# Expert-gate one-hots with two tokens innermost instead of four, in a two-block transformer kernel on one core

## The chip, the cores and the metric

The kernel runs on one core of a Trainium2 chip. It is one program for two transformer blocks, 256 tokens of width 1024 in float32. The metric is the device time of one execution in microseconds (us), the median of three runs.

## What is computed

The first block has two gated feed-forward parts around a mixer (block-sparse attention and retention), the second a mixer (RWKV-7 and mLSTM) and then PEER, a retrieval of single-neuron experts. The change lies in PEER. Cut to what matters:

```python
def _peer(h, w_q, sub_keys, u_emb, v_emb):
    q = (tok @ w_q).reshape(n_tok, 8, 2, 128)
    s = jnp.einsum('nhpc,hpkc->nhpk', q, sub_keys)
    s_top, i_top = lax.top_k(s, 16)
    cand = s_top[:, :, 0, :, None] + s_top[:, :, 1, None, :]
    cand_idx = i_top[:, :, 0, :, None] * 128 + i_top[:, :, 1, None, :]
    best, pos = lax.top_k(cand.reshape(n_tok, 8, 256), 16)
    expert = jnp.take_along_axis(cand_idx.reshape(n_tok, 8, 256), pos, axis=-1)
    gate = jax.nn.softmax(best, axis=-1)
    act = gelu(einsum('tkd,td->tk', u_emb[expert], tok)) * gate
    return einsum('tk,tkd->td', act, v_emb[expert])
```

Each token picks 16 experts in each of 8 heads, 128 of 16384 in all. An expert's number is a pair (a, b) of numbers below 128.

## The kernel before

The kernel does not gather experts. It computes the product of every token with all 16384 rows of `peer_u`, applies GELU, multiplies each product by the token's gate for that expert (zero for most), and multiplies the result by all of `peer_v`.

A float32 weight is split on its way in: a DMA from SyncE's queue brings `raw`, ScalarE rounds it to `whi` (L111), GpSimd and VectorE subtract to get the remainder `wlo` (L113, L115). A product is then three matmuls, L132 to L134, with 256 moving columns each. `pair` does two blocks of 128 experts: 48 such matmuls.

`retrieve` runs in three parts. First come the scores (L1400 to L1411). The searches for the top 16 (`half`, `whole`, L1322 to L1336) and the picks of the winners' numbers (`gates`, `pick`, `turn`, L1338 to L1374) stand in a list of background work, `self.bg`, of which `wload` issues an item after each weight. Third, as soon as the numbers are there (`finish`), the loop over `peer_u` (L1420) also makes the gates: `IT` holds for each token, transposed, the numbers a and b and the gate of its 128 selections, one selection per partition, and `ix` the same in fp16, the gate in two halves (high and low).

For each group of `GT` = 4 tokens, `onehots` (L1385) makes with four VectorE operations of 128x512 elements the one-hots of a and of b (L1391: compare a constant `io`, which counts 0 to 127, with `ix`), and then the one-hot of b times each half of the gate (L1393). Both inputs and the output are fp16. The tile `oh` lies as [what, group, number 0 to 127, token], the token innermost. For each token two matmuls (L1440) sum the product of a's one-hot (the weights, stationary) and b's scaled one-hot (moving, 128 columns) over the selections into `pg`: the 128x128 gates of this token. So there are 512 such gate matmuls, 8 for each group, and their operands step over `oh` by four elements. VectorE (L1443) multiplies the gates into `act`; ScalarE (L1444) copies those for experts still to come. `oh` has two buffers, so VectorE can make a group's one-hots only when the gate matmuls of the group two before are done.

A scheduler sets the order on each engine from a cost estimate of each instruction and from priorities; weights have a lead (`LEAD`). The order of instructions around the change is its result.

Of the kernel before, what the change touches and what calls it, by code (L numbers as in the profile page):

```python
# [12 lines left out]
F16 = mybir.dt.float16  # L13
# [17 lines left out]
GT = 4  # L31
# [36 lines left out]
class K:  # L68
# [406 lines left out]
    def mixer1(self, cx, p, a, b, gate):  # L475
# [101 lines left out]
        onsa = self.new_split(p, [128, 4, T], "on")  # L577
        G = range(2)
        for tt in range(2):
# [6 lines left out]
            for m in range(4):  # L586
                for g in G:
                    nc.tensor.matmul(sc[:, g, m * 16:m * 16 + 16], qh(g, m), kk[64 * g:64 * g + 64, 512:528],
                                     start=m == 0, stop=False, skip_group_check=True)
            mc = self.masks[:, 256 + 16 * tt:272 + 16 * tt]  # L590
            for g in G:
                nc.tensor.matmul(sc[:, g, 0:64], self.idb, mc[:, None, :].to_broadcast([128, 4, 16]), start=False, stop=True,
# [12 lines left out]
            for m in range(4):  # L605
                sc = ps2.tile([128, 2, 512], F32, name="sc")
                for g in G:
                    k = kk[64 * g:64 * g + 64, 0:512].rearrange("p (b k) -> p b k", b=2)
                    nc.tensor.matmul(sc[:, g, 0:2 * n].rearrange("p (b k) -> p b k", b=2), qh(g, m), k[:, :, 0:n],
                                     start=True, stop=False)  # L610
                for g in G:
                    nc.tensor.matmul(sc[:, g, 0:2 * n].rearrange("p (b k) -> p b k", b=2)[:, :, n - 128:n], self.idb,
# [4 lines left out]
                nc.vector.tensor_scalar(mx, mx, -0.125, None, op0=OP.mult)  # L617
                for g in G:
                    for br in range(2):
# [665 lines left out]
    def retrieve(self, act, tok, raws, pre):  # L1285
        nc, A, tc = self.nc, self.A, self.tc
        NEG = -3.0e38
        with ExitStack() as c1:
            pool = lambda n, b, **k: c1.enter_context(tc.tile_pool(name=n, bufs=b, **k))
            keep, pp = pool("pk", 1), pool("pk2", 2)  # L1290
# [8 lines left out]
            def view(n, dt=F32):  # L1299
                self.at += n  # L1300
                x = flat[:, self.at - n:self.at]
                return x if dt == F32 else x.bitcast(dt)
# [12 lines left out]
            iof = view(128)  # L1315
            nc.sync.dma_start(iof, A["iota"])

            io = keep.tile([128, 128, 4], F16, name="io")
            nc.vector.tensor_copy(io, iof[:, :, None].to_broadcast([128, 128, 4]))
            self.ready = False  # L1320

            def top16(v, i, src, n, z):  # L1322
# [56 lines left out]
                nc.vector.tensor_copy(ix[:, 2, :], IT[:, 2, :])  # L1379
                nc.vector.tensor_sub(ix[:, 3, :], IT[:, 2, :], ix[:, 2, :])  # L1380

            G = GT // 4
            shape = [128, G, 128, 4]

            def onehots(t0):  # L1385

                oh = pp.tile([128, 4, G, 128, 4], F16, name="oh")
                x = lambda i: ix[:, i, t0:t0 + GT].rearrange("p (g t) -> p g t", g=G)[:, :, None, :].to_broadcast(shape)
                iota = io[:, None, :, :].to_broadcast(shape)
                for i in range(2):  # L1390
                    nc.vector.tensor_tensor(oh[:, i], iota, x(i), op=OP.is_equal)  # L1391
                for i in (3, 2):
                    nc.vector.tensor_mul(oh[:, i], oh[:, 1], x(i))  # L1393
                return oh
# [24 lines left out]
            done = 0  # L1419
            for j in range(0, 128, 2):  # L1420
                ps = self.pair(A["peer_u"], j, tok, PU if self.ready else PQ).rearrange("p (j t) -> p j t", j=2)
                a = act[:, j:j + 2, :]
                if done < T:
                    nc.scalar.activation(a[:, :, done:], ps[:, :, done:], AF.Gelu)
                if done:
                    g = pp.tile([128, 2, T], F32, name="ge", tag="q")
                    nc.scalar.activation(g[:, :, 0:done], ps[:, :, 0:done], AF.Gelu)
                    nc.vector.tensor_mul(a[:, :, 0:done], a[:, :, 0:done], g[:, :, 0:done])
                J = j + 2
                if self.ready and JA is None:  # L1430
                    JA = J
                todo = 0 if JA is None else T * (J - JA) // (JB - JA) // GT * GT if J < JB else T
                while done < min(todo, T):
                    if done % GT == 0:
                        oh = onehots(done)
                    pg = psG.tile([128, 4, 128], F32, name="pg")
                    g = done % GT // 4
                    for i in range(4):
                        for l in (3, 2):
                            nc.tensor.matmul(pg[:, i, :], oh[:, 0, g, :, i], oh[:, l, g, :, i], start=l == 3, stop=l == 2)  # L1440
                    pv = pg.rearrange("p t j -> p j t")
                    a = act[:, 0:J, done:done + 4]
                    nc.vector.scalar_tensor_tensor(a, pv[:, 0:J, :], 2.0 ** -10, a, op0=OP.mult, op1=OP.mult)  # L1443
                    nc.scalar.activation(act[:, J:128, done:done + 4], pv[:, J:128, :], AF.Copy, scale=2.0 ** -10)  # L1444
                    done += 4
# [199 lines left out]
```

## Time and profile before

| | us |
|---|---|
| median of 3 runs | 1840.1 (1837.5 to 1842.22) |
| the profiled execution, its own time | 1844.43 |
| span of the profiled execution | 1842.6 |
| TensorE (PE) busy, matmuls | 1732.9 |
| VectorE (DVE) busy | 1254.4 |
| ScalarE (ACT) busy | 889.5 |
| GpSimd (POOL) busy | 833.8 |

The span runs from the first to the last instruction of one profiled execution; its own time contains 1.8 us more. PE stands for the matmuls, PEld for the weight loads, which overlap with them. A matmul's duration in the profile holds its passage through the array and overlaps with that of its neighbours: how fast matmuls follow one another is read from their starts. L1440 is line 1440 of the kernel.

### The profile page before, as it was taken

The numbers are of one execution on the slowest core, as the hardware profiler recorded it, in microseconds if no ns is written. First come the engines' busy times: TensorE is split into PE (matmuls) and PEld (weight loads), VectorE is DVE, ScalarE is ACT, GpSimd is POOL, SyncE is SP. The second block draws the span as 40 slices with busy tenths as digits, with TensorE's granted clock in tenths as the row PEclk, the third lists the DMA queues.
The fourth block names the chain that finished last, engine by engine and source line by source line (L and its number), as shares of the span: only waits on it lengthen the run. The fifth ranks groups of instructions, "written<-read, shape, count | busy, mean of one in ns | idle before, by whom it ended". The sixth has DMA issues, their size and how long they took to land.

```text
span 1842.6 us, 36282 instructions
## 1 busy us (share of the span) xinstructions
PE 1732.9 (94%) x13856; PEld 1608.6 (87%) x13856; DVE 1254.4 (68%) x2559; ACT 889.5 (48%) x1416; POOL 833.8 (45%) x625
## 2 busy tenths in 40 slices
PE   5999989999999989899998979999999999999998
PEld 4999977689899989799998878999999988888886
DVE  8886588777744586865588997777788633434344
ACT  4444444645544456644554334444444445555554
POOL 3444522224555556413444655333333456666664
PEclk9999999999999999999999989999999999999999
DMA  7887778536555645303454435545555566666664
GB/s 264 290 319 243 209 271 282 188 115 198 159 184 180 189 146 153 101 15 106 157 179 143 136 120 164 158 151 159 151 151 157 172 196 192 185 190 186 190 186 137
DMA packets 95928, 325.77 MB, mean 177 GB/s; under 512 B 10505, under 2 KB 18313, under 8 KB 95242
## 3 DMA queue, kind: packets, MB, share of 16 engines
q1 hardware_dynamic: 95466, 322.93, 55.5%
q8 instruction: 108, 1.77, 0.4%
q14 instruction: 66, 0.54, 0.1%
q10 hardware_dynamic: 288, 0.52, 0.1%
HBM read 321.32 MB, written 2.10 MB: 176 GB/s over the span
## 4 chain that ended last, share of the span: by engine, by line
PE 64%; DVE 10%; issue 3%; ACT 2%; POOL 2%; DMA 0%; POOLq 0%; ACTq 0%; DVEq 0%; SPq 0%
PE vacc L1469 20%; PE acc L134 12%; PE acc L133 12%; PE acc L132 12%; PE pg L1440 3%; DVE wlo L115 2%; PE pt L908 1%; POOL wlo L113 1%; ACT whi L111 1%; DVE nt L264 1%; DVE rt L753 1%; PE acc L154 0%; DVE cv L1203 0%; PE pt L469 0%; PE pc L1409 0%
## 5 line engine op out<-in xcount | busy, mean ns | idle before, releaser
L113 POOL TENSOR_TENSOR wlo<-raw,whi 128x256 fp32r<-128x256 f32 (+4 forms) x526 | 764.4, 1455 | 847.0 <-ACT whi L111 794.8
L111 ACT CAST whi<-raw 128x1024 fp32r<-128x1024 f32 (+2 forms) x530 | 550.7, 1041 | 434.5 <-PE acc L133 189.2
L134 PE MATMUL acc<-uh,wlo 128*128 128x256 f32 x2352 | 667.7, 284 | 25.2 <-POOL wlo L113 22.1
L115 DVE TENSOR_TENSOR wlo<-raw,whi 128x768 fp32r<-128x768 f32 (+5 forms) x530 | 484.6, 916 | 286.2 <-ACT whi L111 285.2
L132 PE MATMUL acc<-uh,whi 128*128 128x256 f32 x2352 | 670.5, 285 | 1.5 <-DVE gf L439 1.3
L133 PE MATMUL acc<-ul,whi 128*128 128x256 f32 x2352 | 666.7, 283 | 1.3 <-DVE ul L177 1.3
L134 PEld LDWEIGHTS acc<-uh,wlo 128*128 128x128 f32 x2352 | 449.1, 191 | 31.2 <-POOL wlo L113 25.2
L132 PEld LDWEIGHTS acc<-uh,whi 128*128 128x128 f32 x2352 | 451.8, 192 | 3.8 <-DVE gf L439 2.0
L133 PEld LDWEIGHTS acc<-ul,whi 128*128 128x128 f32 x2352 | 450.2, 191 | 3.2 <-DVE ul L177 1.7
L1469 PE MATMUL vacc<-whi,ah 128*128 128x512 f32 x512 | 162.7, 399 | 3.9 <-ACT ah L176 3.9
L1469 PE MATMUL vacc<-whi,al 128*128 128x512 f32 x512 | 162.5, 398 | 0.0
L1469 PE MATMUL vacc<-wlo,ah 128*128 128x512 f32 x512 | 162.4, 398 | 0.0
L177 DVE TENSOR_TENSOR al<-act,ah 128x256 fp32r<-128x256 f32 x128 | 54.7, 429 | 133.9 <-PE vacc L1469 133.4
L176 ACT CAST ah<-act 128x256 fp32r<-128x256 f32 x128 | 52.4, 411 | 158.3 <-PE vacc L1469 156.3
L1469 PEld LDWEIGHTS vacc<-whi,ah 128*128 128x128 f32 x512 | 97.1, 190 | 26.8 <-ACT ah L176 4.1
L1469 PEld LDWEIGHTS vacc<-wlo,ah 128*128 128x128 f32 x512 | 97.1, 190 | 23.1 <-POOL wlo L113 0.2
L1469 PEld LDWEIGHTS vacc<-whi,al 128*128 128x128 f32 x512 | 97.0, 190 | 22.8
L347 DVE SCALAR_TENSOR_TENSOR junk<-aw,cb 128x1024 bf16<-128x1024 f32 x72 | 95.1, 1321 | 11.7 <-DMA aw<-in_ada_w_dram 11.2
L1391 DVE TENSOR_TENSOR oh<-io,ix 128x512 f16<-128x512 f16 x128 | 73.8, 616 | 42.9 <-PE pg L1440 42.9
L132 PE MATMUL acc<-gh,whi 128*128 128x256 f32 x352 | 97.2, 276 | 0.0
L133 PE MATMUL acc<-gl,whi 128*128 128x256 f32 x352 | 97.2, 276 | 0.0
L134 PE MATMUL acc<-gh,wlo 128*128 128x256 f32 x352 | 97.2, 276 | 0.0
(502 smaller groups left out, 2362.1 us busy)
## 6 DMA issues: line engine op xcount, KB each, us to landing
raw<-in_peer_u_dram SPq DMA_DIRECT2D x128, 512.0 KB, 3.6
raw<-in_peer_v_dram SPq DMA_DIRECT2D x128, 512.0 KB, 4.2
raw<-in_ffn_w_in_dram SPq DMA_DIRECT2D x88, 512.0 KB, 3.8
raw<-in_w_in_dram SPq DMA_DIRECT2D x78, 512.0 KB, 3.6
aw<-in_ada_w_dram SPq DMA_DIRECT2D x72, 512.0 KB, 5.6
raw<-in_ffn_w_out_dram SPq DMA_DIRECT2D x32, 448.0 KB, 3.9
raw<-in_ffn_w_out_dram SPq DMA_DIRECT2D x16, 512.0 KB, 3.5
raw<-in_w_out_dram SPq DMA_DIRECT2D x16, 512.0 KB, 3.6
```

Source lines behind the costliest of these rows:

```text
L111: nc.scalar.copy(hi, t)
L113: nc.gpsimd.tensor_sub(lo[:, :pool], t[:, :pool], hi[:, :pool].bitcast(F32))
L115: nc.vector.tensor_sub(lo[:, pool:], t[:, pool:], hi[:, pool:].bitcast(F32))
L132: mm(out, w.hi, x.hi, start=start, stop=False)
L133: mm(out, w.hi, x.lo, start=False, stop=False)
L134: mm(out, w.lo, x.hi, start=False, stop=stop)
L176: self.nc.scalar.copy(hi, src)
L177: self.nc.vector.tensor_sub(lo, src, hi.bitcast(F32))
L347: nc.vector.scalar_tensor_tensor(self.junk, t, 1.0, self.cb, op0=OP.mult, op1=OP.mult, accum_out=acc)
L1391: nc.vector.tensor_tensor(oh[:, i], iota, x(i), op=OP.is_equal)
L1440: nc.tensor.matmul(pg[:, i, :], oh[:, 0, g, :, i], oh[:, l, g, :, i], start=l == 3, stop=l == 2)
L1469: nc.tensor.matmul(acc[2 * tt + d], x[:, ts], y[:, d * 512:(d + 1) * 512], start=j == 0 and x is a.hi and y is w.hi, stop=j == 127 and x i ...
```

## The change

The innermost dimension of the one-hots becomes two tokens instead of four. A group of 4 tokens (`GT` stays 4) is now two sub-groups of two: `oh` lies as [what, sub-group, number, token of the pair]. The constant `io` has two copies of each number in place of four, and the matmuls pick sub-group and token with `divmod`. Sizes and counts of the one-hot operations and of the matmuls stay; what a matmul steps over is two elements (4 bytes) instead of four (8 bytes), and `io` is read twice over by each compare.

```diff
-            io = keep.tile([128, 128, 4], F16, name="io")
-            nc.vector.tensor_copy(io, iof[:, :, None].to_broadcast([128, 128, 4]))
+            io = keep.tile([128, 128, 2], F16, name="io")
+            nc.vector.tensor_copy(io, iof[:, :, None].to_broadcast([128, 128, 2]))
...
-            G = GT // 4
-            shape = [128, G, 128, 4]
+            G = GT // 2
+            shape = [128, G, 128, 2]
...
-                oh = pp.tile([128, 4, G, 128, 4], F16, name="oh")
+                oh = pp.tile([128, 4, G, 128, 2], F16, name="oh")
...
-                    g = done % GT // 4
                     for i in range(4):
+                        g, t = divmod(done % GT + i, 2)
                         for l in (3, 2):
-                            nc.tensor.matmul(pg[:, i, :], oh[:, 0, g, :, i], oh[:, l, g, :, i], start=l == 3, stop=l == 2)
+                            nc.tensor.matmul(pg[:, i, :], oh[:, 0, g, :, t], oh[:, l, g, :, t], start=l == 3, stop=l == 2)
```

On PE, ScalarE and SyncE's queue the order of instructions is the same as before, and on VectorE from the first one-hot (L1391) on. On VectorE it differs ahead of that, from the cast of `io` on. There VectorE did in this order (MAX, MAX_INDEX and MATCH_REPLACE are the searches, L115 a weight's remainder; `act` holds their scratch space):

```order
L115 TENSOR_TENSOR wlo<-raw,whi 128x256
L1319 CAST io<-act 128x512
L1326 MAX act<-act 128x8
L115 TENSOR_TENSOR wlo<-raw,whi 128x256
L1327 MAX_INDEX act<-act 128x8
L1323 MAX act<-act 128x8 x2
```

Now it does, on the same engine at the same place:

```order
L115 TENSOR_TENSOR wlo<-raw,whi 128x256
L1319 CAST io<-act 128x256
L1326 MAX act<-act 128x8
L1323 MAX act<-act 128x8
L115 TENSOR_TENSOR wlo<-raw,whi 128x256
L1327 MAX_INDEX act<-act 128x8
```

The cast has half the elements, and one search operation stands ahead of the next weight's remainder. Such exchanges of a weight's remainder with one or two searches follow in a dozen places. On VectorE at the start of the picks the difference reads (L1363 compares positions, L1349 to L1352 end the softmax of the gates):

```order
 L1349 CAST act<-act 128x128
 L1351 RECIPROCAL act<-act 128x8
+L1363 TENSOR_TENSOR act<-act 128x512
 L115 TENSOR_TENSOR wlo<-raw,whi 128x256
 L1352 TENSOR_TENSOR act<-act 128x128
```

A pick's first operation has moved ahead of a weight's remainder, and the picks behind it are dealt out among the weights by other steps.

## Rows read from the trace of the kernel before

**Rows 1.** The page, part 1: busy us, share of the span, instructions

```profile
PE 1732.9 (94%) x13856; PEld 1608.6 (87%) x13856; DVE 1254.4 (68%) x2559; ACT 889.5 (48%) x1416; POOL 833.8 (45%) x625
```

**Rows 2.** Windows: length, busy PE PEld DVE ACT POOL (instructions), PEclk, DMA share, GB/s

```profile
980.00:1060.00 80.00, 71.49 (x567) 69.00 (x565) 78.14 (x366) 31.64 (x38) 46.38 (x34) 0.96 0.43 133
1060.00:1127.00 67.00, 50.72 (x367) 49.02 (x367) 61.57 (x112) 24.08 (x30) 39.83 (x24) 0.87 0.41 127
1127.00:1443.00 316.00, 315.61 (x2726) 312.75 (x2725) 248.96 (x459) 141.60 (x247) 106.20 (x95) 1.00 0.52 156
```

**Rows 3.** The chain that ended last, of the stretch 1127 to 1443 us

```profile
by line: PE acc L134 26.9%; PE acc L132 26.8%; PE acc L133 26.8%; PE pg L1440 19.2%; DVE wlo L115 0.3%; DVE oh L1393 0.1%; issue 0.0%
```

**Rows 4.** Waits, 1127 to 1443 us: total us, times, longest

```profile
DVE oh L1391 <- PE pg L1440: 42.9, 43, 1.8
...
DVE wlo L115 <- ACT whi L111: 23.7, 28, 2.0
```

**Rows 5.** Timeline of PE around three bursts: start, us, what (merged where alike)

```profile
1139.53 1.11 PE L1440 MATMUL pg<-oh 128*128 128x128 f16 x8
...
1255.69 0.28 PE L133 MATMUL acc<-ul,whi 128*128 128x256 f32 x1
1255.81 0.28 PE L134 MATMUL acc<-uh,wlo 128*128 128x256 f32 x1
1255.92 1.11 PE L1440 MATMUL pg<-oh 128*128 128x128 f16 x8
1256.79 0.37 PE L132 MATMUL acc<-uh,whi 128*128 128x256 f32 x1
1256.99 0.28 PE L133 MATMUL acc<-ul,whi 128*128 128x256 f32 x1
...
1441.20 2.06 PE L1440 MATMUL pg<-oh 128*128 128x128 f16 x16
```

**Rows 6.** All that touches the tile oh: duration ns min/median/max

```profile
L1440 PEld LDWEIGHTS <-oh x512: 112/117/138, 1139.5 to 1442.8; 128*128 128x128 f16 x171
L1440 PE MATMUL pg<-oh x512: 283/297/303, 1139.5 to 1443.0; 128*128 128x128 f16 x171
L1391 DVE TENSOR_TENSOR oh<-io,ix x128: 406/426/965, 1127.5 to 1436.3; 128x512 f16<-128x512 f16 x128
L1393 DVE TENSOR_TENSOR oh<-oh,ix x128: 403/412/976, 1130.9 to 1439.5; 128x512 f16<-128x512 f16 x128
```

**Rows 7.** Timeline of PE: the 16-bit mask matmuls, operands side by side

```profile
287.10 0.20 PE L592 MATMUL sc<-masksb,idb 128*128 128x64 bf16 x1
...
287.14 0.20 PE L592 MATMUL sc<-masksb,idb 128*128 128x64 bf16 x1
...
287.37 0.28 PE L134 MATMUL acc<-uh,wlo 128*128 128x256 f32 x1
...
290.49 0.28 PE L612 MATMUL sc<-masksb,idb 128*128 128x256 bf16 x1
...
290.61 0.27 PE L612 MATMUL sc<-masksb,idb 128*128 128x256 bf16 x1
...
290.85 0.28 PE L134 MATMUL acc<-uh,wlo 128*128 128x256 f32 x1
```

**Rows 8.** Line 612: the weight load of a side-by-side 16-bit operand

```profile
L612 PEld LDWEIGHTS <-idb x16: 95/97/99, 290.5 to 343.3; 128*128 128x128 bf16 x16
```

**Rows 9.** Line 1363: an f32 operation of the same width on VectorE

```profile
L1363 DVE TENSOR_TENSOR act<-act x16: 675/682/2317, 1070.0 to 1119.2; 128x512 f32<-128x512 f32 x16
```

**Rows 10.** Line 1319: the cast of the constant io

```profile
L1319 DVE CAST io<-act x1: 2055/2055/2055, 983.4 to 983.4; 128x512 f16<-128x512 f32 x1
```

**Rows 11.** Waits of PE, 980 to 1127 us: total us, times, longest

```profile
PE acc L134 <- POOL wlo L113: 21.6, 9, 4.4
```

**Rows 12.** Timeline of PE: 64-column f32 matmuls of the second mixer

```profile
819.24 0.87 PE L908 MATMUL pt<-idn,X 64*64 64x64 f32 x24
```

**Rows 13.** Line 908: their weight loads

```profile
L908 PEld LDWEIGHTS pt<-idn,X x256: 129/135/135, 801.2 to 822.9; 64*64 64x64 f32 x128
```

## The prediction

> **What bounds the kernel now.** I read the page's totals first: PE is busy 94% of the span [rows 1]. That share is an average, so next comes the table of windows [rows 2]. The reader should look at two of its stretches. From 1127 to 1443 us, where the expert gates are applied, PE is busy 315.6 of 316.0 us at a granted clock of 1.00 (the 2.4 GHz level), VectorE 249.0, and the DMA share is 0.52. From 980 to 1127 us, the top-16 searches and picks, VectorE is busy 78.1 of 80.0 and 61.6 of 67.0 us while PE has gaps and a clock of 0.96 and 0.87. So the one-hot stage is bound by PE, the stage ahead of it mostly by VectorE. The chain of waits of the one-hot stage says the same: four lines of PE make up all but half a per cent of it, and the gate matmuls (L1440) alone are 19.2%, or 60.7 us, 0.119 us for each of 512 [rows 3]. The other engines wait for PE or for each other there [rows 4]. A nanosecond off each gate matmul is therefore half a microsecond off the kernel.
>
> **Why the gate matmuls cost that.** The timeline of PE shows them in 45 bursts, the first at 1139.53 us and the last at 1441.20, of 8 or 16 matmuls each [rows 5]. A burst of 8 lasts 1.11 us and one matmul alone 0.297 [rows 5, 6], so the seven spacings are (1.11 - 0.297) / 7 = 0.116 us; the burst of 16 gives (2.06 - 0.297) / 15 = 0.1175. I take 0.117. The f32 matmuls around them start every 0.11 us with 256 moving columns; the gate matmuls have 128 columns and take as long. The trace has 16-bit matmuls with operands that lie side by side: with 64 columns two start 0.04 us apart, with 256 columns 0.12 us [rows 7]. That is 0.08 us for 192 columns, 0.42 ns each, plus a fixed 0.013. For 128 columns this line gives 0.013 + 128 x 0.417 ns = 0.066 us. So the gate matmuls take 0.051 us more than their columns explain. What is special about them is the step: neighbouring columns of a one-hot lie 4 elements, 8 bytes, apart. A gate matmul thus reads across 128 x 8 = 1024 bytes per partition, exactly what an f32 matmul reads with 256 x 4, and their spacings agree. That is my reason to think that the bytes passed over set the pace, not the columns.
>
> **The change, part by part.**
> 1. *Matmuls.* Counts and order on PE stay; the step falls from 8 to 4 bytes, so the 128 columns lie within 512 bytes. Four bytes per column is what the f32 matmuls have at 0.42 ns per column. The price of a 16-bit matmul with a 4-byte step is in no row. Bounds: from below half an f32 spacing, 0.057 us; from above no gain, 0.117. I take 0.066, the value of the side-by-side rows, since those are the nearest in type. Inside the bursts there are 512 - 45 = 467 spacings: 467 x 0.051 = **23.8 us**, all on the chain.
> 2. *Back to f32.* From the start of a burst's last matmul (1255.92 + 7 x 0.117 = 1256.74) to the second f32 matmul (1256.99) pass 0.25 us [rows 5]; behind the side-by-side 16-bit pairs it is 0.23 and 0.24 [rows 7]. 45 x 0.015 = **0.7 us**. The first spacing of a burst belongs to the f32 matmul ahead of it and stays.
> 3. *Weight loads.* A one-hot load lasts 117 ns [rows 6], a side-by-side one 97 [rows 8]. Whether that matters is rival B.
> 4. *VectorE, one-hots.* 256 operations of 128x512 as before, median 426 and 412 ns [rows 6]; only the patterns change, with rows of two elements instead of four. I cost that at nothing: an operation of this width at one element per cycle takes 675 ns [rows 9], so these run at two, and a pair is still adjacent. From the first one-hot on the order of VectorE is the same. The cover is PE: with its stage at 316 - 24.5 = 291.5 us, VectorE has 249.0 busy and 23.7 of waits for weight casts [rows 4], 272.7 together. The 42.9 us in which it waited for gate matmuls to free a one-hot buffer are what shrinks. 19 us of room are left.
> 5. *The iota cast.* It halves from 512 elements, now 2.06 us [rows 10], in the stage that VectorE bounds: between 0 and 1.0 us gained. I take 0.
> 6. *The order ahead.* The shorter cast lets the scheduler move the weight subtractions (L115) by a place or two among the searches, and one pick (L1363) ahead of one of them. PE waited there 21.6 us for weights in 9 waits, the longest 4.4 [rows 11]. One wait more or one fewer is up to 4.4 us either way; I take 0.
>
> The sum is 23.8 + 0.7 = **24.5 us**. The profiled execution took 1844.4 us and would take 1819.9; the median of the three runs is 4.3 us lower, and against it I predict 1840.1 - 24.5 = **1815.6 us**. DMA has room for a stage 8% shorter: its share there is 0.52.
>
> **A rule that speaks against it.** The gate matmuls now are at 0.117 us where side-by-side columns give 0.066. The Trainium skill, page "SBUF — State Buffer", section "Door 1: The DMA port swizzle", says that two hits on a 16-byte line suffice for full bandwidth, so that 8 elements of bf16 can be stepped over for free. By that rule a step of 4 already costs nothing and the change brings nothing: 1840.1 us. The trace does not agree that the present step is free, unless something else slows these matmuls; so the rule is rival C. The same notes, page "TensorE: Matmul & The Clock Gate", section "Back-to-back issue gap", put pairs of load and matmul with 128 columns at about 81 ns; by that the first term would be an estimated 467 x 0.036 = 16.8 us.
>
> **The rivals.**
> *B, the weight load takes over.* In a burst the loads last 117 ns, the same as the spacing; if each matmul must wait for a whole load, the spacing falls only to the 97 ns of a side-by-side load: 467 x 0.020 = 9.3 us, 1830.8. Against it: 24 of the 64-column f32 matmuls run within 0.87 us, at most 36 ns each, while one load is 135 ns long [rows 12, 13]; but those alternate between two halves of the array, so it is not excluded.
> *C, no change.* Any step other than one, or fp16 itself, may run at half rate; nothing in the trace has a step of two. Then 1840.1 us, give or take the 4.4 us of term 6.
> *D, slower: VectorE drops to one element per cycle* because the repeated row is now only one pair long. Price: 675 - 412 = 0.26 us on each of 256 one-hot operations, 66.6 us. VectorE's 272.7 us become 339.3, more than the 316 of the stage: 1840.1 + 23.3 = 1863.4 us. It decides from (291.5 - 272.7) / 256 = 73 ns extra per operation, where it begins to eat the gain; above (316 - 272.7) / 256 = 169 ns the kernel is slower than before. For it: no row of the trace shows rows of two 16-bit elements. Against it: rows of four run at full rate. The Trainium skill, page "Vector Engine (DVE) Microarchitecture Reference", section 5.1, says that two elements per partition do run at double rate and that a row read again and again does too; no run here shows it yet.
>
> **How the numbers follow.** The forecast has 0.62, B 0.14, C 0.14, D 0.10. A measurement of this kernel can tell about 0.3%, 5.5 us, from no change. The forecast and B are faster, and a small part of C by the order ahead: 0.77. The rest of C is the same: 0.13. D is slower: 0.10. The forecast's own range is 1810 (a spacing of 0.057, 4 us less, and a little from term 6) to 1824 (a spacing of 0.075 with one more weight wait). To leave out no more than 2 in 10, the range goes up over B and half of C: 1810 to 1841.
>
> **What would show it.** Right: 8 gate matmuls from first start to f32 restart in about 0.5 us instead of 0.87 [rows 5], spacings near 0.066, the one-hot stage near 291 us, their share of its chain near 12%, VectorE's wait for gate matmuls about halved with its operations still at 410 to 430 ns, one-hot loads under 117 ns. B shows as spacings of 0.097; C as 0.117; D as one-hot operations near 680 ns and PE waiting for weights from L115. Wrong altogether would be a stage no shorter although the spacings fell: then a VectorE or weight wait has taken their place.

## The result and the profile after

The changed kernel takes **1809.5 us** (median of 4 runs, 1807.8 to 1810.9) where the kernel before took 1840.3 beside it (median of 4, 1837.5 to 1842.2): a ratio of 0.982, 95% interval 0.980 to 0.984. The gain is 30.8 us; 24.5 had been forecast, and the time lies half a microsecond below the lower end of the range. The profiled execution took 1807.8 us, 1.7 under its median (the one before had been 4.1 over its own).

The page of the changed kernel opens with its span (1842.6 us before) and the busy time of the engines, which answers to [rows 1]:

```profile
span 1806.0 us, 36282 instructions
...
PE 1695.2 (94%) x13856; PEld 1575.8 (87%) x13856; DVE 1255.9 (70%) x2559; ACT 887.1 (49%) x1416; POOL 828.8 (46%) x625
```

The counts of instructions are those of before on every engine. PE is busy 37.7 us less, VectorE as long as before. Where that happened is in the windows (columns as in [rows 2]; the last window ends where the last burst now ends):

```profile
980.00:1060.00 80.00, 70.98 (x587) 68.58 (x585) 77.26 (x379) 33.20 (x41) 47.28 (x36) 1.00 0.46 141
1060.00:1127.00 67.00, 51.73 (x371) 50.17 (x370) 61.78 (x106) 24.01 (x30) 39.51 (x22) 0.87 0.41 126
1127.00:1413.00 286.00, 284.50 (x2718) 282.03 (x2717) 251.19 (x457) 138.58 (x245) 99.76 (x93) 1.00 0.56 172
```

The stage in which the gates are applied is over after 286 us instead of 316, at the same granted clock of 1.00, and PE is still busy in all but 1.5 us of it. The two search windows in front look as before, but for the clock of the first (1.00 instead of 0.96). So the stage shrank because its own bound shrank; no wait of PE went away, and only 1.3 us of waits came in its place. The tile of the one-hots [rows 6] shows on what:

```profile
L1440 PEld LDWEIGHTS <-oh x512: 96/97/102, 1139.1 to 1412.9; 128*128 128x128 f16 x171
L1440 PE MATMUL pg<-oh x512: 217/218/233, 1139.1 to 1413.0; 128*128 128x128 f16 x171
L1391 DVE TENSOR_TENSOR oh<-io,ix x128: 407/416/983, 1127.0 to 1409.0; 128x512 f16<-128x512 f16 x128
L1393 DVE TENSOR_TENSOR oh<-oh,ix x128: 404/410/1001, 1130.4 to 1411.7; 128x512 f16<-128x512 f16 x128
```

A gate matmul lasts 218 ns instead of 297, its weight load 97 instead of 117, and the one-hot operations of VectorE take 410 to 416 ns, where they took 412 to 426. In the timeline of PE (start, duration, what), around the burst that answers to the one at 1255.92 in [rows 5]:

```profile
1256.43 0.28 PE L134 MATMUL acc<-uh,wlo 128*128 128x256 f32 x1
1256.55 0.63 PE L1440 MATMUL pg<-oh 128*128 128x128 f16 x8
1256.99 0.36 PE L132 MATMUL acc<-uh,whi 128*128 128x256 f32 x1
1257.19 0.29 PE L133 MATMUL acc<-ul,whi 128*128 128x256 f32 x1
```

From the first gate matmul to the return of f32 pass 0.44 us instead of 0.87. Over all bursts, read from the starts of the single matmuls in the two traces, the 467 spacings inside bursts sum to 28.4 us where they were 54.7; the median spacing is 57 ns, against 118 (means 61 and 117). The chain of waits from 1139 to 1413 us and the waits from 1127 to 1413 us (us in total, times, longest) answer to [rows 3, 4]:

```profile
by line: PE acc L132 28.8%; PE acc L133 28.0%; PE acc L134 27.9%; PE pg L1440 10.3%; DVE oh L1391 1.4%; issue 1.1%; DVE oh L1393 0.9%; DVE act L1428 0.7%; DVE act L1443 0.6%; ACT whi L111 0.4%; DVE wlo L115 0.2%
```

```profile
DVE wlo L115 <- ACT whi L111: 21.6, 26, 1.7
DVE oh L1391 <- PE pg L1440: 12.3, 18, 1.0
```

The gate matmuls' share of the chain fell from 19.2% to 10.3%, 28.2 of 274 us. VectorE waits 12.3 us for a one-hot buffer instead of 42.9. Busy time and its wait for weights are 251.2 + 21.6 = 272.8 us of the 286.0: the room of a dozen microseconds is what is left before VectorE becomes the bound here. That room is an average over the stage, and near its end it is gone. From 1386 to 1400 us the chain runs over ScalarE and VectorE, and in the bursts at 1392.8 and 1399 us three spacings last 331, 466 and 332 ns, about 0.9 us lost to one-hots that come late (each time the next gate matmul starts some 50 ns behind the end of an operation of L1393):

```profile
1388.07 1.84 DVE oh L1391 x2
...
1395.04 1.29 DVE oh L1393 x2
```

```profile
1399.88 0.89 PE L1440 MATMUL pg<-oh 128*128 128x128 f16 x8 [0.25 <-DVE oh L1393]
```

The other traces with two tokens innermost in both operands (e0, e1, e4 and e9 below) have such pauses at the same place.

**Where the 36.6 us between the two profiled spans lie.** The first gate matmul starts at 1139.07 us instead of 1139.53: 0.5 us. From there to the last gate matmul 273.9 us pass instead of 303.4: 29.5 us. From there to the end 393.0 instead of 399.7: 6.7 us, in a part that the change does not touch. The median moved by 30.8 only, so these last 6.7 us call for another execution of the kernel before (experiment e6_before).

The 29.5 us of the stage divide, by the same starts, into 26.3 inside the bursts; 1.1 at the return to f32 (from the start of a burst's last matmul to the second f32 matmul 227 ns instead of 252, 44 times within the stage); and 2.1 in the f32 matmuls between the bursts, whose mean spacing fell from 114.8 to 113.8 ns. That last part was in no term of the sum. Here is a stretch between two bursts in each timeline, the kernel before first:

```profile
1243.02 0.28 PE L133 MATMUL acc<-ul,whi 128*128 128x256 f32 x1
1243.13 0.28 PE L134 MATMUL acc<-uh,wlo 128*128 128x256 f32 x1
...
1248.43 0.28 PE L134 MATMUL acc<-uh,wlo 128*128 128x256 f32 x1
```

The changed kernel:

```profile
1244.88 0.28 PE L134 MATMUL acc<-uh,wlo 128*128 128x256 f32 x1
1244.99 0.28 PE L132 MATMUL acc<-uh,whi 128*128 128x256 f32 x1
...
1249.98 0.28 PE L134 MATMUL acc<-uh,wlo 128*128 128x256 f32 x1
```

Before, 46 spacings take 5.41 us, 117.6 ns each; now 45 take 5.10 us, 113.3 each, for the same instructions at the same granted clock. A stretch of 48 f32 matmuls between two bursts keeps the one pace or the other to its end. Of the 44 stretches, 13 were slow before; 1 is now.

### The profile page after: what moved, and what is told of

It is laid out like the page before. It is cut to its first block, busy times and chain, and to the rows that moved or that the text cites. A ratio compares the mean times of both kernels' runs of the same rounds, so it can differ in the third digit from the quotient of the medians.

```text
span 1806.0 us, 36282 instructions
## 1 busy us (share of the span) xinstructions
PE 1695.2 (94%) x13856; PEld 1575.8 (87%) x13856; DVE 1255.9 (70%) x2559; ACT 887.1 (49%) x1416; POOL 828.8 (46%) x625
## 4 chain that ended last, share of the span: by engine, by line
PE 61%; DVE 15%; issue 3%; ACT 2%; POOL 2%; DMA 1%; POOLq 0%; ACTq 0%; DVEq 0%; SPq 0%
PE vacc L1469 20%; PE acc L132 11%; PE acc L133 11%; PE acc L134 11%; DVE wlo L115 3%; PE pg L1440 2%; PE pt L908 1%; POOL wlo L113 1%; ACT whi L111 1%; DVE act L1327 1%; DVE act L1325 1%; DVE act L1324 1%; DVE nt L264 1%; PE pt L469 1%; DVE act L1326 1%
## 5 line engine op out<-in xcount | busy, mean ns | idle before, releaser
L115 DVE TENSOR_TENSOR wlo<-raw,whi 128x768 fp32r<-128x768 f32 (+5 forms) x530 | 492.3, 930 | 280.9 <-ACT whi L111 279.8
L1469 PEld LDWEIGHTS vacc<-whi,ah 128*128 128x128 f32 x512 | 96.5, 189 | 24.5 <-ACT ah L176 4.1
L1391 DVE TENSOR_TENSOR oh<-io,ix 128x512 f16<-128x512 f16 x128 | 61.8, 521 | 12.6 <-PE pg L1440 12.3
```

What stands on the lines that cost most here:

```text
L115: nc.vector.tensor_sub(lo[:, pool:], t[:, pool:], hi[:, pool:].bitcast(F32))
L1469: nc.tensor.matmul(acc[2 * tt + d], x[:, ts], y[:, d * 512:(d + 1) * 512], start=j == 0 and x is a.hi and y is w.hi, stop=j == 127 and x i ...
```

## The experiments

Theory: the moving operand's step sets the pace of a gate matmul. Against it stood rival B (the pace is that of the weight load, whose operand changed its step too), the order ahead (the changed order on VectorE in front of the stage gives or takes a part), and, for the size, what exactly the step costs. Diffs are against the changed kernel.

**e0_after.** The changed kernel again, as the measure for the next three.

> The changed kernel once more, for a second profile beside the same runs of the kernel before. Median 1809.5 us, within 2 us. If the spacing of the 512-column matmuls of the value product (0.234 us in the profile before, 0.230 in the one after) belongs to the change, it is 0.230 again; if it is a matter of the single execution, it may stand anywhere from 0.226 to 0.234.

Measured: 1810.7 us (5 runs, 1807.5 to 1819.3), ratio 0.983 [0.981, 0.986] to the kernel before, which took 1841.9 beside it. From first to last gate matmul 274.0 us, median spacing 57 ns, 1 slow f32 stretch of 44: the stage in the trace after is typical. The 512-column matmuls of the value product are 230 ns apart again.

**e1_four_copies.** The constant `io` keeps four copies, so that its cast and the order of VectorE ahead are those of the kernel before; the one-hots have two tokens innermost.

```diff
-            io = keep.tile([128, 128, 2], F16, name="io")
-            nc.vector.tensor_copy(io, iof[:, :, None].to_broadcast([128, 128, 2]))
+            io = keep.tile([128, 128, 4], F16, name="io")
+            nc.vector.tensor_copy(io, iof[:, :, None].to_broadcast([128, 128, 4]))
...
-                iota = io[:, None, :, :].to_broadcast(shape)
+                iota = io[:, None, :, 0:2].to_broadcast(shape)
```

> Two tokens innermost in the one-hots, but the constant io keeps its four copies, so that the cast and the order on every engine are those of before. If the new order and the shorter cast are worth nothing, the time is that of the changed kernel, 1809.5 us. If the part of the gain that the gate matmuls do not explain comes from the searches, as the two traces suggest with some 3 us there, it is 1812 to 1814 us. Gate spacing 0.057 us in either case.

Measured: 1812.4 us (1809.0 to 1815.0), ratio 0.983 [0.981, 0.985]; the stage 274.1 us, spacing 57 ns. All but 1.7 us of the gain is there without the changed order ahead. The time lies in the band expected for a part from the searches, but these 1.7 us to e0_after lie within the scatter of both.

**e2_moving_two and e3_weights_two** part the two operands of the gate matmul. In e2 the weights (`oh[0]`) keep four tokens innermost and the moving operands have two, in e3 the other way round. `io` keeps four copies in both, so their measure is e1.

```diff
+                def lay(i):
+                    n = 4 if i == 0 else 2
+                    s = [128, 4 // n, 128, n]
+                    o = oh[:, i].rearrange("p (g k t) -> p g k t", g=4 // n, t=n)
...
-                        g, t = divmod(done % GT + i, 2)
+                        gw, tw = divmod(done % GT + i, 4)
+                        gm, tm = divmod(done % GT + i, 2)
...
-                            nc.tensor.matmul(pg[:, i, :], oh[:, 0, g, :, t], oh[:, l, g, :, t], start=l == 3, stop=l == 2)
+                            nc.tensor.matmul(pg[:, i, :], oh[0][:, gw, :, tw], oh[l][:, gm, :, tm], start=l == 3, stop=l == 2)
```

(e3: `n = 2 if i == 0 else 4`, and 2 and 4 exchanged in the two `divmod` lines.)

> Only the moving one-hots (of b) have two tokens innermost; the stationary ones (of a) keep four. If the step of the moving operand sets the pace, the spacing is 0.057 us with weight loads still near 0.115 us, and the time is that of the kernel with four copies of io. If the weight load sets it, the spacing stays near 0.115 us and the time near 1840 us.

> The mirror image: only the stationary one-hots have two tokens innermost, the moving ones keep four. If the step of the moving operand sets the pace, the spacing stays at 0.107 to 0.117 us though a load falls to 0.097, and the time is within 5 us of 1840. If the weight load sets it, the spacing is 0.057 to 0.066 us and the time that of the kernel with four copies of io.

The tile of the one-hots in e2, then in e3:

```profile
L1447 PEld LDWEIGHTS <-oh x512: 112/113/137, 1141.3 to 1416.5; 128*128 128x128 f16 x171
L1447 PE MATMUL pg<-oh x512: 217/221/253, 1141.3 to 1416.6; 128*128 128x128 f16 x171
```

```profile
L1447 PEld LDWEIGHTS <-oh x512: 95/116/120, 1143.1 to 1442.8; 128*128 128x128 f16 x171
L1447 PE MATMUL pg<-oh x512: 275/297/300, 1143.1 to 1443.0; 128*128 128x128 f16 x171
```

Measured: e2 1812.2 us (6 runs, 1805.5 to 1821.3), ratio 0.984 [0.981, 0.987]; e3 1836.1 us (8 runs, 1829.5 to 1837.7), ratio 0.995 [0.994, 0.997]. In e2 the loads take 113 ns, nearly as long as before, and the matmuls follow each other every 59 ns: a load twice as long as the spacing holds nothing up. In e3 the matmuls are back at a median spacing of 117 ns, and the loads beside them mostly at 116, not at the expected 97, although their own step is the short one. So the moving operand sets the pace and the load does not, and rival B falls. A load is long from either cause: from its own step of four beside quick matmuls (e2), or beside matmuls of a step of four (e3). e3 is not quite the kernel before, though: it gains 5.8 us. Its trace shows none of the 44 f32 stretches slow (e2: 5), some 2.5 us, and 1.0 us less inside the bursts (mean spacing 115.0). Its stage is 3.6 us shorter than that of the profile before; the other 2.2 us of the medians are not placed. Two tokens innermost in the weights alone thus have a small effect, and most of what the traces place of it lies in the f32 matmuls behind the bursts rather than in the gate matmuls.

**e4_steps.** Between the one-hot stage and the value product, bursts of 16 matmuls on zeros, each with one step of the moving or the weight operand; nothing reads their result. A few of the 16 bursts:

```diff
+            self.steps()
...
+            [mm(o[:, 0:128], w[:, 0:128], z[:, 0:128], start=True, stop=True) for _ in R]
+            [mm(o[:, 0:128], w[:, 0:128], z[:, 0:256:2], start=True, stop=True) for _ in R]
+            [mm(o[:, 0:128], w[:, 0:128], z[:, 0:384:3], start=True, stop=True) for _ in R]
...
+            [mm(o[:, 0:128], w[:, 0:128], z[:, 0:2048:16], start=True, stop=True) for _ in R]
...
+            [mm(o[:, 0:128], w[:, 0:2048:16], z[:, 0:128], start=True, stop=True) for _ in R]
```

> The changed kernel with bursts of 16 matmuls of zeros set between the gates and the value product (some 25 us more; they add nothing to the output): 128 fp16 columns, weights and moving operand each at steps of 1, 2, 3, 4, 6, 8 and 16 elements, and bf16 at steps of 2 and 4. If the bytes that the moving operand passes over set the pace (1024 bytes in 0.107 us), the spacings are 0.057, 0.057, 0.083, 0.110, 0.163, 0.217 and 0.430 us. If it is lines of 16 bytes, the first six are the same and step 16 is 0.217 us again. If any step over two runs at half rate, steps 3 to 16 are all near 0.110 us. With the weights stepped and the moving columns side by side the spacing stays at 0.057 us up to a step of 4 if the moving operand sets the pace. bf16 as fp16.

Measured: steps of 3, 4 and 6 gave 88, 116 and 171 ns, and bf16 at steps of 2 and 4 gave 58 and 116, so fp16 has no part in it. Steps of 8 and 16 gave 227 and 232, but the granted clock was 0.5 (the 1.2 GHz level) from 1454.4 to 1464.7 us, which takes in these two bursts, all but the start of the first, and the weights' steps of 2 and 4. PE had been busy without a gap when it fell. The bursts of steps 8 and 16, and a window in them (columns as in [rows 2]):

```profile
1453.98 3.81 PE L1465 MATMUL zo<-zz,zw 128*128 128x128 f16 x16
1457.61 3.89 PE L1466 MATMUL zo<-zz,zw 128*128 128x128 f16 x16
```

```profile
1454.50:1461.30 6.80, 6.80 (x31) 3.70 (x30) 0.00 (x0) 0.00 (x0) 0.00 (x0) 0.50 0.00 0
```

The first burst, at step 1, and most of the second ran at 0.5 as well, at 107 ns. So the run leaves open what the clock did to these spacings.

**e9_steps_full_clock.** The same with bursts of 12, each led by 24 matmuls of 512 columns that lie side by side.

```diff
+            R, mm = range(12), nc.tensor.matmul
+            [mm(o, w[:, 0:128], z[:, 0:512], start=True, stop=True) for _ in range(24)]
+            [mm(o[:, 0:128], w[:, 0:128], z[:, 0:128], start=True, stop=True) for _ in R]
+            [mm(o, w[:, 0:128], z[:, 0:512], start=True, stop=True) for _ in range(24)]
+            [mm(o[:, 0:128], w[:, 0:128], z[:, 0:256:2], start=True, stop=True) for _ in R]
...
```

> The bursts of zeros again (they add nothing to the output), 12 matmuls each, now with 24 side-by-side matmuls of 512 columns ahead of every burst, since in the first such run the granted clock fell to 0.5 at steps 8 and 16 and at two of the weight steps. At a clock of 1.0 throughout: if the pace is one 16-byte line in some 1.8 ns, moving steps 1, 2, 3, 4, 6, 8, 16 give 0.057, 0.057, 0.088, 0.116, 0.171, 0.227 and 0.23 us; if it is bytes, step 16 gives 0.43. If the 0.227 of step 8 came from the low clock, it is near 0.12 now. Weights at steps 2, 4, 8 and 16 with side-by-side moving columns: 0.057 to 0.062 us each if the weight load does not set the pace; up to 0.117 and more if it does.

The window of the bursts (columns as in [rows 2]):

```profile
1458.00:1540.00 82.00, 81.85 (x460) 42.74 (x458) 0.00 (x0) 0.00 (x0) 0.00 (x0) 1.00 0.00 1
```

The clock is 1.00 throughout. The bursts in the timeline of PE, in order: moving operand at steps 1, 2, 3, 4, 6, 8, 16 (weights side by side); weights at steps 2, 4, 8, 16 (moving operand side by side); weights 4 with moving 2; weights 2 with moving 4:

```profile
1460.52 0.83 PE L1459 MATMUL zo<-zz,zw 128*128 128x128 f16 x12
1466.37 0.85 PE L1461 MATMUL zo<-zz,zw 128*128 128x128 f16 x12
1472.24 1.22 PE L1463 MATMUL zo<-zz,zw 128*128 128x128 f16 x12
1478.48 1.55 PE L1465 MATMUL zo<-zz,zw 128*128 128x128 f16 x12
1485.05 2.22 PE L1467 MATMUL zo<-zz,zw 128*128 128x128 f16 x12
1492.29 2.88 PE L1469 MATMUL zo<-zz,zw 128*128 128x128 f16 x12
1500.19 2.94 PE L1471 MATMUL zo<-zz,zw 128*128 128x128 f16 x12
1508.15 0.83 PE L1473 MATMUL zo<-zz,zw 128*128 128x128 f16 x12
1514.00 0.83 PE L1475 MATMUL zo<-zz,zw 128*128 128x128 f16 x12
1519.85 0.90 PE L1477 MATMUL zo<-zz,zw 128*128 128x128 f16 x12
1525.77 0.92 PE L1479 MATMUL zo<-zz,zw 128*128 128x128 f16 x12
1531.70 0.88 PE L1481 MATMUL zo<-zz,zw 128*128 128x128 f16 x12
1537.60 1.56 PE L1483 MATMUL zo<-zz,zw 128*128 128x128 f16 x12
```

Each duration holds 11 spacings and one whole matmul. The spacings themselves, from the single starts, beside what the 128 columns touch in a partition:

| step of the moving operand | 1 | 2 | 3 | 4 | 6 | 8 | 16 |
|---|---|---|---|---|---|---|---|
| bytes passed over | 256 | 512 | 768 | 1024 | 1536 | 2048 | 4096 |
| 16-byte lines touched | 16 | 32 | 48 | 64 | 96 | 128 | 128 |
| spacing, ns | 56 | 58 | 88 | 116 | 171 | 227 | 232 |

From step 3 on the spacing is 1.8 ns per 16-byte line. From step 8 to 16 the bytes double, the lines do not, and neither does the time. So the pace is that of lines, not of bytes passed over (steps between 8 and 16 were not tried), and at steps 1 and 2 the columns are the bound: twice the lines cost 2 ns there. Put beside e4, the table says one thing more: steps 8 and 16 took the same 227 and 232 ns at half the granted clock, while side-by-side columns took 107 ns there and 56 here. The pace by columns follows the clock of TensorE, the pace by lines does not. A step of two is as good as none, and a step of four costs a factor of two. The weights' step does next to nothing: 56, 56, 62 and 63 ns at steps 2, 4, 8 and 16. Weights at 4 with moving columns at 2 take 60 ns, the other way round 116: what e2 and e3 showed, without one-hots.

**e5_one_token.** One token innermost: the one-hots lie side by side. This looks for the point where rival D begins.

```diff
-            io = keep.tile([128, 128, 2], F16, name="io")
-            nc.vector.tensor_copy(io, iof[:, :, None].to_broadcast([128, 128, 2]))
+            io = keep.tile([128, 128, 1], F16, name="io")
+            nc.vector.tensor_copy(io, iof[:, :, None])
...
-            G = GT // 2
-            shape = [128, G, 128, 2]
+            G = GT
+            shape = [128, G, 128, 1]
...
-                        g, t = divmod(done % GT + i, 2)
+                        g, t = divmod(done % GT + i, 1)
```

> One token innermost: the columns of a one-hot lie side by side, and each row of the repeated operand of the one-hot operations is a single element. If the step still costs something at two, the spacing falls below 0.057 us; if columns already set the pace at a step of two, it stays there. If a single repeated element makes VectorE do one element per cycle, the one-hot operations take near 0.68 us, VectorE bounds the one-hot stage at 330 to 340 us and the kernel takes 1855 to 1875 us; if they stay at 0.41 us, the time is that of the changed kernel within 3 us.

The tile of the one-hots, the window of the stage and the longest wait of PE in it:

```profile
L1440 PE MATMUL pg<-oh x512: 216/219/230, 1138.8 to 1461.9; 128*128 128x128 f16 x171
L1391 DVE TENSOR_TENSOR oh<-io,ix x128: 672/678/1227, 1126.7 to 1457.0; 128x512 f16<-128x512 f16 x128
L1393 DVE TENSOR_TENSOR oh<-oh,ix x128: 674/683/1259, 1129.0 to 1460.7; 128x512 f16<-128x512 f16 x128
```

```profile
1127.00:1462.00 335.00, 302.32 (x2736) 294.71 (x2735) 325.59 (x459) 139.79 (x246) 105.16 (x93) 0.98 0.48 148
```

```profile
PE pg L1440 <- DVE oh L1393: 29.8, 31, 2.3
```

Measured: 1858.6 us (6 runs, 1849.6 to 1869.5), ratio 1.010 [1.007, 1.014]: slower than the kernel before. The gate matmuls are no quicker (median spacing 56 ns against 57), but the one-hot operations take 678 and 683 ns, the time of one element per cycle [rows 9]. VectorE is busy 325.6 of 335.0 us, and PE waits 29.8 us for one-hots. Rival D is a real mechanism of this kernel with the price that was set on it (0.26 us each); it begins at one element innermost, not at two. The Trainium skill, page "Vector Engine (DVE) Microarchitecture Reference", section 5.1, lists among the conditions of double rate for 16-bit operands more than one element innermost: 416 ns with two and 678 with one agree. With one token innermost the repeated operand is also a single element read 128 times in a row, and this run does not part the two.

**e6_before.** The kernel before, once more, for the 6.7 us behind the last gate matmul.

> The kernel before once more, for a second profile of it. If its 512-column matmuls of the value product are 0.234 us apart again, the 6.6 us by which that stage differs between the two profiles belong to the change; if they are 0.230, to the first profile alone, which was 4 us above its median. The f32 spacing of the one-hot stage (0.1148 us in the first profile, 0.1138 in the changed kernel) likewise.

Measured: 1834.6 us in one execution. From first to last gate matmul 304.1 us (303.4 in the profile before), from the last to the end 393.1 instead of 399.7. In the value product, two matmuls of 512 columns at a time, the profile before, then e6:

```profile
1599.67 0.63 PE L1469 MATMUL vacc<-wlo,ah 128*128 128x512 f32 x2
1600.14 0.63 PE L1469 MATMUL vacc<-whi,al 128*128 128x512 f32 x2
```

```profile
1599.69 0.62 PE L1469 MATMUL vacc<-wlo,ah 128*128 128x512 f32 x2
1600.15 0.62 PE L1469 MATMUL vacc<-whi,al 128*128 128x512 f32 x2
```

The first execution spaced them by 234 ns on average, this one by 230, as do the two of the changed kernel (after, e0); e9, built on the changed kernel, has 233. So the slower pace is not tied to the kernel before, and the 6.7 us are not a gain of the change; how often either kernel runs at it, these few traces do not tell. The stage's length belongs to the kernel: e6 repeats it, with 16 of 44 f32 stretches slow.

**e7_old_step_small_io.** The other half of e1: the order ahead and the small constant of the changed kernel, with four tokens innermost as before.

```diff
-            G = GT // 2
-            shape = [128, G, 128, 2]
+            G = GT // 4
+            shape = [128, G, 128, 4]
...
-                iota = io[:, None, :, :].to_broadcast(shape)
+                iota = io[:, :, None, :].to_broadcast([128, 128, 2, 2])
...
-                        g, t = divmod(done % GT + i, 2)
...
-                            nc.tensor.matmul(pg[:, i, :], oh[:, 0, g, :, t], oh[:, l, g, :, t], start=l == 3, stop=l == 2)
+                            nc.tensor.matmul(pg[:, i, :], oh[:, 0, g, :, i], oh[:, l, g, :, i], start=l == 3, stop=l == 2)
```

> The one-hots as before, four tokens innermost, but the constant io with two copies, so that the cast and the order of VectorE and GpSimd ahead of the one-hots are those of the changed kernel. If the order and the cast are what the searches gained, this kernel has them and nothing else: 2 to 3 us under the kernel before, with gates 0.117 us apart. If that gain came from elsewhere, it is the same as before within 1 us.

Measured: 1839.8 us (12 runs, 1836.6 to 1845.8) beside 1840.8 for the kernel before (17 runs), ratio 0.9993 [0.9979, 1.0006]. The order ahead is worth at most 3.9 us (the interval's lower end), and nothing is resolved. In the traces the way from the first score matmul to the first gate matmul is 163.2 us on average in the five with the old order (162.2 to 164.4), and 161.5 in the six with the new one (161.1 to 162.0). That is 1.6 us, and the 1.7 us between e1 and e0 and the 1.0 us here point the same way, but as a time it stays open.

## Why the prediction was wrong in size and right in kind

The direction, the bound and the mechanism held, in that the moving operand's step sets the pace; the forecast's own case is what happened. Two terms were too small and one was missing, together enough to leave the range by 0.5 us, which is less than the scatter of the runs. The range had allowed 4 us for a spacing of 0.057, and the bursts took 2.5 of them; without the missing term, the f32 matmuls of number 4, the time would have been some 1811.6 us and inside.

1. **Matmuls: the step that was sized wrong.** "I take 0.066, the value of the side-by-side rows, since those are the nearest in type." The spacing is 0.057, which the text had as its lower bound. The line through the side-by-side rows [rows 7] had a fixed part of 0.013 us, taken from pairs of matmuls alone between f32 work and from starts printed to 0.01 us. In a burst the spacing side by side is 56 ns (e9), and 128 columns at the 0.417 ns of the same line are 53.4, so the fixed part is some 3 ns. A pair holds only the first spacing behind f32 work, and that one is longer in the changed kernel's bursts as well: 71 ns in the median. With the median of all, 57, the term would be 28 us; with these first spacings and the 0.9 us of late one-hots the sum over all 467 fell by 26.3 instead of 23.8.
2. **The reason behind it** was wrong as well: not the bytes passed over but the 16-byte lines touched set the pace (e9). Up to a step of eight elements, bytes and lines grow together, so for a step of 4 against 2 both give half, and the wrong reason cost nothing here.
3. **Back to f32**: 1.1 us against 0.7.
4. **The f32 matmuls between the bursts: the step that failed.** The forecast put them at nothing without a reason; they gave 2.1 us. Why is open. The two paces, 114 and 118 ns, were to be seen in the trace of before, and they bound the term: 13 slow stretches of 46 spacings at 4 ns are 2.4 us.
5. **Weight loads, rival B**: next to no effect on the spacing, as taken (59 ns in e2, 60 in e9). That the load's 117 ns equalled the spacing meant nothing: with its step of four a load takes 113 ns beside quick matmuls too (e2).
6. **One-hots on VectorE at nothing**: right for the operations, 416 and 410 ns against 426 and 412. Busy time and weight waits of 272.8 us are what the sum said (272.7). The room of 19 us, 13 as it came out, was an average, though, and did not cover the end of the stage, where 0.9 us were lost.
7. **The iota cast**: the bound of 0 to 1.0 us held, near its lower end. Half the elements take nearly as long:

```profile
L1319 DVE CAST io<-act x1: 1922/1922/1922, 985.1 to 985.1; 128x256 f16<-128x256 f32 x1
```

It took 2.06 us before [rows 10], so 0.13 us came off.
8. **The order ahead at nothing**: right within what can be told (e1, e7). PE's wait for weights in the searches is unchanged against [rows 11]:

```profile
PE acc L134 <- POOL wlo L113: 21.7, 9, 4.6
```

The two rules that had been set against the trace fail here. The Trainium skill, page "SBUF — State Buffer", section "Door 1: The DMA port swizzle", lets 16-bit operands be stepped over by 8 for free and so would have given no change (rival C): 58, 116 and 227 ns at steps of 2, 4 and 8 contradict it for a matmul's moving operand. Two columns per line are half the pace, four are enough. The estimate of 16.8 us by 81 ns per pair (the Trainium skill, page "TensorE: Matmul & The Clock Gate", section "Back-to-back issue gap") is off in the other direction: pairs of load and matmul with 128 columns follow each other every 56 ns in e9.

The sum after the fact: 26.3 + 1.1 + 2.1 = 29.5 us from the traces, against 30.8 in the medians. The remaining 1.3 us lie where the order ahead may have given something and where one execution differs from the next; they were not settled.

## What to carry to other kernels

When a matmul takes longer than its columns explain, look at how many 16-byte lines of a partition its moving operand touches: 128 columns of 16 bits are free of cost up to a step of two, and twice as slow at four. The layout that suits the matmul has to be weighed against the engine that writes it: here two elements innermost serve both, while one element halves VectorE's rate and loses more than all that was gained. And a fixed cost read from an isolated pair of instructions can be too high for a sustained burst, as here (13 ns against 3): take such a row as a bound.

## What the runs showed of the hardware that was not expected

- **A matmul's moving operand is read by 16-byte lines at 1.8 ns each** (88 ns for 48 lines, 116 for 64, 171 for 96, 227 for 128), and TensorE's granted clock does not change that (227 ns at 0.5 in e4 and at 1.00 in e9). The f32 matmuls of this kernel fit the same pace: 256 columns are 64 lines and take 113 to 118 ns, 512 columns are 128 lines and take 230, whereas 24 side-by-side 16-bit matmuls of 512 columns (64 lines) run from 1461.19 to 1466.37 us in e9, 216 ns each. That f32 is bound by its lines is argued from these numbers and was not tried by itself.
- **The weight operand's step hardly matters**: 56 to 63 ns per matmul from step 1 to step 16, and a load of 113 ns is hidden at a spacing of 59.
- **A stretch of f32 matmuls has two paces, 114 and 118 ns, and how often the slow one comes goes with the layout of the one-hots.** Slow were 13, 16 and 17 of 44 stretches in the three traces with a step of four on both operands (before, e6, e7), 5 with it on the weights alone (e2), none with it on the moving operand alone (e3), and 1 or 2 with a step of two on both. A shorter step is not what decides: with one token innermost (e5) 29 of the 45 stretches of more than 20 f32 matmuls were slow. What chooses, and why the choice holds for 48 matmuls, was not found.
